# Transposes of B's probabilities put ahead of C's last score product in the mixers' tails, and the experts' gate products run without interruption

## The chip, the cores and the metric

The kernel runs on one core of a Trainium2 chip. The metric is the device time of one execution in microseconds (us). An engine is named by its short name: PE is TensorE (matrix products and transposes), DVE VectorE, ACT ScalarE, POOL GpSimd, SP SyncE, which here only issues DMAs. PSUM is the memory that PE writes its results to; DVE and ACT read them from there.

## The reference: two layers of three attentions and a mixture of experts

The sequence has 256 tokens of width 1024. Each of the two layers does this, all in fp32:

```
mod = silu(c) @ ada_w[l] + ada_b[l]          # six vectors sh1 sc1 g1 sh2 sc2 g2
h = rmsnorm(x) * (1 + sc1) + sh1
proj = h @ w_in[l]                           # columns for three groups of heads
  A: differential attention, 4 heads         # softmax - lam * softmax, then a norm
  B: sliding window of 128, 8 heads on 2 kv heads, with sinks
  C: mixture of three dilated windows, 4 heads
x = x + g1 * (concat(A, B, C) @ w_out[l])
h = rmsnorm(x) * (1 + sc2) + sh2
# router: the best of 4 groups, in it the best 2 of 4 experts, per token
x = x + g2 * sum over the chosen experts of  gate * (silu(h @ wg) * (h @ wu)) @ wd
```

After the layers comes a last norm. There are 16 experts with 1024 x 512 matrices, so the weights (283.63 MB are moved in all) have to come from HBM once.

## The kernel before: one written order for PE, a ring of weight tiles, and a scheduler for the rest

**Weights.** SP issues all weight loads in one fixed sequence (class Ring, the DMAs stand at L154). Most go into 29 buffers of 512 KB called `big`, a few into borrowed `k` or `w` tiles of the kernel's other pools. A load can be issued when the buffer that it goes into has been read by its last user, mostly a PE product, and up to eight loads are under way at a time.

**PE's order is written by hand** (`tc.manual_schedule` for PE). For a mixer it is a string of steps, one list for each layer (MIX), with a common end (TAIL):

- `Pug` is a unit of the projection by w_in, `W0` to `W6` the units of the product with w_out. Both are done as three products of high and low parts of the operands (L724 to L726); ACT makes the high part of a weight by a cast (L776), DVE the low part by a subtraction (L781, one takes 1.2 us).
- For the three groups of heads: `T` transposes queries and keys, `F` makes scores (L1081 for B and C), `V` transposes probabilities (L809), `O` is the product with the values (L890, L893), `AM` transposes A's result (copies L1057, L1058). `CT0` and `CT1` are the transposes of C's queries and keys, whose results ACT and DVE copy (L1074, L1075). `BV0` and `BV1` are the first two transposes of probabilities, `CF0` and `CF1` C's two score steps.
- Behind a score step comes the softmax: DVE masks and takes maxima (L835, reads the scores), negates them (L839, tile `nm`), ACT makes exponentials (L841), DVE takes a reciprocal of the sums (L854) and POOL scales (L857). ACT copies the transposed probabilities (L866) and the products with the values (L896, which W2 needs).
- `a` and `d` are parts of the products of c with ada_w (L462, L537). Of two of these results the columns are taken later by four transposes (L480) and adds (L491 to L494); L551 and L555 are the like for `d`.

The order of DVE, ACT and POOL is not written: a scheduler decides it from PE's order and its own durations. Where two steps share a PSUM buffer (there are two called `t` for transposes and two called `s` for scores), the later one waits until the earlier one has been read.

**The router's bias** is two small products (L603, L604) behind W1, copied by DVE (L606).

**The experts** are done in eight pairs, j = 0 to 7. For an even j, `gather` (L1338) picks the tokens of two pairs by one-hot products in four parts, and ACT and DVE modulate them (L730, L732). For each j come the gate products (L1372, 32 matmuls in four parts of 8), `down` of the pair before (L1418, 32), the up products (L1372, 32), the product of the two (L1403) and `combine` of the pair before (L1439, added to x by L1441). `down_in` is the four transposes (L809) with a copy (L1409) that bring the product into the form that `down` needs. `one_hot` (L1314) makes the one-hot matrices on DVE.

## Time and profile before

| what | value |
|---|---|
| three runs | 746.42, 746.60, 748.49 us (median 746.6) |
| the profiled execution | 746.45 us |
| its span, from the first to the last instruction | 744.6 us |
| busy in the span | PE 708.5 us, DVE 343.4, ACT 213.4, POOL 62.4 |
| moved by DMA | 283.63 MB, 381 GB/s over the span |

The time that lies outside the span is 1.85 us. Layer 0's mixer runs to about 160 us, its experts to 380, layer 1's mixer to about 512, its experts to 730. A view of the timeline lists instructions by their start on one engine, and in brackets how long the engine was idle before and what it waited for; in the chain of waits each line is a stretch of the chain that ended last.

### The profile page before, as it was taken

What the parts mean: (1) busy time and instruction counts of PE and PEld (TensorE: products, weight loads), DVE (VectorE), ACT (ScalarE), POOL (GpSimd) and SP (SyncE); (2) the same over time, 40 slices, a digit from 0 to 9 for tenths busy, and PEclk for the clock granted to TensorE, in tenths of its full rate; (3) what the DMA queues carried; (4) which work ended last, traced back from release to release, by engine and by line L of the source; (5) the groups of instructions that cost most, each with busy time, mean ns of one, the idle gap of its engine ahead of it and who ended that gap; (6) DMA issues with size and microseconds to landing.
All of it is one profiled execution on the core that took longest, in us unless ns stands there. A gap on an engine that the chain in (4) does not pass through costs nothing. (4 is left out here: it accounts for less than half of the span.)

```text
span 744.6 us, 10676 instructions
## 1 busy us (share of the span) xinstructions
PE 708.5 (95%) x3790; PEld 369.1 (50%) x3790; DVE 343.4 (46%) x941; ACT 213.4 (29%) x485; POOL 62.4 (8%) x86
## 2 busy tenths in 40 slices
PE   6899998999999999999999999898999999999993
PEld 2565765764353353353347678575435335344341
DVE  4677796364132233133358879737313312332234
ACT  2445445433111110111134555644211011111012
POOL 1011234001000000000001121400100000000001
PEclk9899999899999999999999999999999999999998
DMA  9999999999989999999999996969899999999991
GB/s 352 409 409 407 407 408 409 407 387 408 406 349 409 409 410 408 409 409 410 399 406 409 405 407 224 354 218 405 315 358 403 406 409 409 409 409 409 409 386 65
DMA packets 82457, 283.63 MB, mean 381 GB/s; under 512 B 9166, under 2 KB 9295, under 8 KB 82396
## 3 DMA queue, kind: packets, MB, share of 16 engines
q1 hardware_dynamic: 82186, 282.85, 96.7%
q8 instruction: 32, 0.52, 0.3%
q14 instruction: 29, 0.24, 0.1%
q0 software_dynamic: 64, 0.02, 0.0%
q10 hardware_dynamic: 146, 0.00, 0.0%
HBM read 281.78 MB, written 1.06 MB: 380 GB/s over the span
## 5 line engine op out<-in xcount | busy, mean ns | idle before, releaser
L1372 PE MATMUL s<-big,k 128*64 128x512 f32 x976 | 228.2, 598 | 0.0
L1372 PEld LDWEIGHTS s<-big,k 128*64 128x64 f32 x976 | 67.3, 136 | 118.6 <-issue 103.8
L1424 DVE SCALAR_TENSOR_TENSOR w<-acc,gs,g 128x512 f32<-128x512 f32 x28 | 21.0, 751 | 155.3 <-PE acc L1418 153.8
L1418 PE MATMUL acc<-big,w 128*64 128x512 f32 x384 | 84.4, 592 | 0.0
L781 DVE TENSOR_TENSOR k<-big,k 128x1024 fp32r<-128x1024 f32 (+1 forms) x56 | 66.8, 1201 | 14.3 <-ACT k L776 10.5
L724 PE MATMUL acc<-k 128*128 128x512 f32 (+1 forms) x176 | 69.9, 397 | 2.9 <-ACT k L713 2.0
L725 PE MATMUL acc<-k 128*128 128x512 f32 (+1 forms) x176 | 66.4, 377 | 0.0
L726 PE MATMUL acc<-k 128*128 128x512 f32 (+1 forms) x176 | 66.4, 377 | 0.0
L776 ACT CAST k<-big 128x1024 fp32r<-128x1024 f32 (+1 forms) x56 | 54.1, 983 | 38.9 <-PE acc L725 27.5
L1418 PEld LDWEIGHTS acc<-big,w 128*64 128x64 f32 x384 | 27.6, 137 | 54.8 <-issue 52.5
L1403 DVE TENSOR_TENSOR w<-w,s 128x512 f32<-128x512 f32 x16 | 11.0, 687 | 82.8 <-PE s L1372 82.8
L1428 ACT CAST w<-w 128x512 fp32r<-128x512 f32 x28 | 17.3, 618 | 89.8 <-DVE w L1424 89.8
L724 PEld LDWEIGHTS acc<-k 128*128 128x128 f32 x176 | 33.8, 192 | 17.9 <-issue 6.9
L841 ACT ACTIVATE w<-w,nm 128x128 f32<-128x128 f32 (+1 forms) x80 | 35.4, 444 | 21.4 <-DVE nm L839 21.4
L1338 PEld LDWEIGHTS t<-w,k 128*128 128x128 f32 x256 | 32.8, 190 | 16.3 <-issue 9.9
L1409 ACT COPY w<-t 128x512 f32<-128x512 f32 x16 | 9.3, 584 | 106.4 <-PE t L809 106.4
L1338 PE MATMUL t<-w,k 128*128 128x256 f32 x256 | 37.6, 291 | 1.7 <-DVE w L1314 1.7
L730 ACT ACTIVATE k<-t,mod,mod 128x256 f32<-128x256 f32 x32 | 16.3, 559 | 77.3 <-PE t L1338 77.3
L726 PEld LDWEIGHTS acc<-k 128*128 128x128 f32 x176 | 33.7, 192 | 7.4 <-DVE k L897 1.4
L809 PE MATMUL t<-cb,w 128*128 128x128 f32 x224 | 35.2, 287 | 2.1 <-ACT w L866 1.1
L725 PEld LDWEIGHTS acc<-k 128*128 128x128 f32 x176 | 33.9, 193 | 5.0
L1441 DVE TENSOR_TENSOR x<-x,acc 128x512 f32<-128x512 f32 x56 | 34.9, 683 | 0.2
(272 smaller groups left out, 851.1 us busy)
## 6 DMA issues: line engine op xcount, KB each, us to landing
big<-in_expert_w_up_dram SPq DMA_DIRECT2D x126, 512.0 KB, 10.2
big<-in_expert_w_gate_dram SPq DMA_DIRECT2D x118, 512.0 KB, 10.2
big<-in_expert_w_down_dram SPq DMA_DIRECT2D x108, 512.0 KB, 10.1
big<-in_ada_w_dram SPq DMA_DIRECT2D x80, 512.0 KB, 10.2
big<-in_w_in_dram SPq DMA_DIRECT2D x32, 512.0 KB, 10.2
big<-in_ada_w_first_dram SPq DMA_DIRECT2D x16, 512.0 KB, 10.2
big<-in_w_out_dram SPq DMA_DIRECT2D x16, 512.0 KB, 9.5
w<-in_expert_w_down_dram SPq DMA_DIRECT2D x20, 256.0 KB, 5.9
```

What stands on the lines that cost most here:

```text
L724: self.nc.tensor.matmul(p, lhsT=xh, rhs=wh, start=start, stop=False)
L725: self.nc.tensor.matmul(p, lhsT=xh, rhs=wl, start=False, stop=False)
L726: self.nc.tensor.matmul(p, lhsT=xl, rhs=wh, start=False, stop=stop)
L776: nc.scalar.copy(hi, w)
L781: nc.vector.tensor_tensor(out=lo, in0=w, in1=hi.bitcast(F32), op=OP.subtract)
L809: self.nc.tensor.transpose(p[:, i], b, self.ident)
L841: nc.scalar.activation(e[:, h], e[:, h], AF.Exp, bias=nm[:, g:g + 1], scale=scale, accum_out=sm[:, g:g + 1])
L1338: nc.tensor.matmul(p[:, kk], lhsT=part[t][:, 2 * k2 + kk], rhs=one[:, t], start=(n == 0), stop=(n == 3))
L1372: nc.tensor.matmul(store[j][64 * u:64 * u + 64, :], lhsT=x[k // 4][:, k % 4, c:c + 64], rhs=w[u][kk], start=(k == 0), stop=(k == KT - 1))
L1418: nc.tensor.matmul(ps[hf][64 * u:64 * u + 64, :], lhsT=act[j][:, f, 64 * u:64 * u + 64], rhs=w[u][hf], start=(f == 0), stop=(f == 3))
L1424: nc.vector.scalar_tensor_tensor(out=ds[-1], in0=p, scalar=gates[j], in1=g[:, 512 * hf:512 * hf + 512], op0=OP.mult, op1=OP.mult)
L1441: nc.vector.tensor_tensor(out=self.x[t][:, c], in0=self.x[t][:, c], in1=p, op=OP.add)
```

## The change

Four things are changed.

- In TAIL, `CT0` and `CT1` leave the tail and go into the string ahead of it (layer 0: behind P40 and P41; layer 1: behind P41 and P43). `CF1` moves from behind W0 to behind `BV0 BV1`. One `d` moves.
- The columns of ada results wait for five flushes instead of two when they belong to the next layer (`later_on`), so layer 0's L480 comes behind W4 instead of W1.
- For the experts, an even j does all four gathers first and then all 32 gate matmuls; `down_in` of a pair runs at the end of its own iteration, behind `combine`, and not between the next pair's gates. j = 0 keeps gathers between gates, and j = 1 keeps `down_in(0)` there.
- `one_hot` for pairs 1, 2, 3 of iterations is issued behind the `places` of the iteration before.

The number of instructions stays the same on every engine.

```diff
 TAIL = """
-CT0 d CT1 d d CF0 AM1 d W0 CF1
-BV0 BV1 W1 BV2 BV3 BO0 BV4 W2 BV5 CV0 W3 BO1 CV1 CV2 W4 CO0 W5 W6
+d d CF0 AM1 d d W0 BV0 BV1 CF1
+W1 BV2 BV3 BO0 BV4 W2 BV5 CV0 W3 BO1 CV1 CV2 W4 CO0 W5 W6
 """
...
-P40 P41 BF1 a P42 AM0 P43 BF2 a a a H2 a
+P40 CT0 P41 CT1 BF1 a P42 AM0 P43 BF2 a a a H2 a
...
-P40 P41 BF1 P42 G2 AM0 P43 BF2 H2
+P40 P41 CT0 BF1 P42 G2 AM0 P43 CT1 BF2 H2
...
-        self.pending.append(lambda: self.pending.append(lambda: self.ada_columns(l, q, rows)))
+        self.later_on(2 if q else 5, lambda: self.ada_columns(l, q, rows))
...
+    def later_on(self, n, f):
+
+        self.pending.append(f if n == 1 else lambda: self.later_on(n - 1, f))
...
             if k2 == 0:
-                if b:
-                    self.one_hot(b)
                 xt[b] = [self.wk.tile([128, 4, S], F32, name="k") for _ in range(2)]
...
-        def gates_of(j, between=None):
-
-            if j % 2:
+        def gates_of(j):
+
+            if j == 0:
+                gather(0, 0)
+                gather(0, 1)
                 first("gate", G, j, 0)
+                gather(0, 2)
                 first("gate", G, j, 1)
-                if between:
-                    between()
+                gather(0, 3)
             else:
-                gather(j // 2, 0)
-                gather(j // 2, 1)
+                for k2 in range(0 if j % 2 else 4):
+                    gather(j // 2, k2)
                 first("gate", G, j, 0)
-                gather(j // 2, 2)
-                if between:
-                    between()
+                if j == 1:
+                    down_in(0)
                 first("gate", G, j, 1)
-                gather(j // 2, 3)
             first("gate", G, j, 2)
             first("gate", G, j, 3)
             silu(j)
...
-            gates_of(j, (lambda: down_in(j - 1)) if j else None)
+            gates_of(j)
...
             places(j)
+            if j in (1, 3, 5):
+                self.one_hot(j // 2 + 1)
...
             elif j:
                 combine(j - 1, *parts)
+                down_in(j)
```

In the order of the changed kernel a line has the number of the new file: L480 to L555 are unchanged, lines of the mixer are 4 higher than here (L781 is L785 there, L835 L839, L841 L845, L866 L870, L896 L900, L1048 L1052, L1075 L1079), lines of the experts 2 higher (L1338 is L1340, L1372 L1374, L1439 L1441).

**End of layer 0's mixer, ACT.** Before, the exponentials of CF1 (L841, four of 128x256) stand ahead of all four copies of BV0 to BV3 (L866), and W2's input (L896) behind these:

```order
57 L776 CAST k<-big 128x1024
58 L841 ACTIVATE w,sm<-w,nm 128x256 x4
59 L866 COPY w<-t 128x512 x4
60 L896 CAST k<-s 128x512
61 L866 COPY w<-t 128x512
```

After:

```order
54 L780 CAST k<-big 128x1024 x2
55 L870 COPY w<-t 128x512 x3
56 L845 ACTIVATE w,sm<-w,nm 128x256 x4
57 L870 COPY w<-t 128x512
58 L900 CAST k<-s 128x512
59 L870 COPY w<-t 128x512
```

Three of the copies have moved ahead of the exponentials, and the exponentials stand nearer to L896.

**Layer 1's mixer, DVE, from P42 on.** Before, the last maxima of BF1 (L835) come first, then one subtraction L781, and then the add L494, which reads the columns of L480:

```order
552 L835 ISA w,mx<-s,cb 128x256
553 L835 ISA mx 128x1
554 L838 TENSOR_TENSOR mx<-mx,sink_339 128x2
555 L623 SCALAR_TENSOR_TENSOR rta<-rya 128x4
556 L781 TENSOR_TENSOR k<-big,k 128x1024
557 L838 TENSOR_TENSOR mx<-mx,sink_339 128x2
558 L839 TENSOR_SCALAR nm<-mx 128x2
559 L624 TENSOR_TENSOR rta<-rta,rma 128x4
560 L494 TENSOR_TENSOR mod_3_4169<-t,cb 128x8
```

After:

```order
547 L628 TENSOR_TENSOR rta<-rta,rma 128x4
548 L629 SCALAR_TENSOR_TENSOR rya<-rta,rya 128x4
549 L785 TENSOR_TENSOR k<-big,k 128x1024
550 L1052 TENSOR_TENSOR w<-w,rya 128x256
551 L1053 TENSOR_TENSOR w<-w,cb 128x256
552 L856 TENSOR_TENSOR sm<-sm,es 128x8
553 L494 TENSOR_TENSOR mod_3_4178<-t,cb 128x8
554 L1079 COPY w<-t 128x2x128
555 L839 ISA w,mx<-s,cb 128x256
```

L494 now has the two products of A's norm (L1052, L1053) ahead of it as well, and BF1's maxima come behind it. Somewhat later in the same order of the changed kernel come the maxima of BF2 (rows 569 on):

```order
563 L858 RECIPROCAL rc<-sm 128x8
564 L785 TENSOR_TENSOR k<-big,k 128x1024
565 L1062 TENSOR_TENSOR w<-t,w 128x2x128
566 L842 TENSOR_TENSOR mx<-mx,sink_339 128x2 x2
567 L785 TENSOR_TENSOR k<-big,k 128x1024 x2
568 L843 TENSOR_SCALAR nm<-mx 128x2 x2
569 L839 ISA w,mx<-s,cb 128x256
570 L839 ISA mx 128x1
571 L1079 COPY w<-t 128x2x128
572 L839 ISA w,mx<-s,cb 128x256
```

Before, two subtractions L781 stand between BF1's maxima and BF2's, and two more behind BF2's; now all four stand ahead of BF2's maxima, three of them in these rows.

**Experts, PE, an even j (here j = 2 of layer 0).** Before:

```order
438 L1439 MATMUL acc<-w 128x512 x8
439 L1338 MATMUL t<-w,k 128x256 x16
440 L1372 MATMUL s<-big,k 64x512 x4
441 L1338 MATMUL t<-w,k 128x256 x8
442 L809 MATMUL t<-cb,w 128x128 x4
443 L1372 MATMUL s<-big,k 64x512 x4
444 L1338 MATMUL t<-w,k 128x256 x8
445 L1372 MATMUL s<-big,k 64x512 x8
446 L1418 MATMUL acc<-big,w 64x512 x16
```

After:

```order
437 L1441 MATMUL acc<-w 128x512 x8
438 L813 MATMUL t<-cb,w 128x128 x4
439 L1340 MATMUL t<-w,k 128x256 x32
440 L1374 MATMUL s<-big,k 64x512 x16
441 L1420 MATMUL acc<-big,w 64x512 x16
```

The work is the same; the gate products (L1372, two trace rows for each of these) now stand in one piece, and the transposes L809 of `down_in` behind `combine` (L1439).

## Rows read from the trace of the kernel before

**Rows 1.** The page: GB/s moved by DMA in 40 slices of 18.6 us.

```profile
GB/s 352 409 409 407 407 408 409 407 387 408 406 349 409 409 410 408 409 409 410 399 406 409 405 407 224 354 218 405 315 358 403 406 409 409 409 409 409 409 386 65
```

**Rows 2.** Stretches: us, busy time by engine (instructions), PE clock, DMA share, GB/s.

```profile
129.60:136.40 6.80, 6.80 (x34) 5.00 (x34) 1.95 (x5) 2.10 (x4) 1.18 (x2) 0.50 1.03 410
...
200.00:220.00 20.00, 20.00 (x106) 9.54 (x102) 7.76 (x15) 4.02 (x8) 0.00 (x0) 1.00 0.89 350
```

**Rows 3.** Timeline of PE, layer 0: W1's start, L480, W2's start.

```profile
123.87 0.47 PE L724 MATMUL acc<-k,w 128*128 128x512 f32 x1
...
128.84 0.66 PE L480 MATMUL t<-cb,w 128*128 128x128 f32 x4 [1.96 <-ACT w L866]
...
135.61 0.78 PE L724 MATMUL acc<-k 128*128 128x512 f32 x1
```

**Rows 4.** Timeline of ACT, layer 0: first exponential of CF1, copies of BV0 and BV1.

```profile
126.24 0.51 ACT L841 ACTIVATE w<-w,nm 128x256 f32<-128x256 f32 x1 [4.39 <-DVE nm L839]
...
128.22 1.04 ACT L866 COPY w<-t 128x512 f32<-128x512 f32 x2
```

**Rows 5.** Timeline of SP's DMA queue, layer 0's experts: two issues in succession.

```profile
200.31 0.33 SPq L154 DMA_DIRECT2D k<-in_expert_w_up_dram  x1
206.09 0.80 SPq L154 DMA_DIRECT2D big<-in_expert_w_up_dram  x2
```

**Rows 6.** Who waited (us, times) for the loads issued from 372 to 385.

```profile
  PEld acc L462: 2.7, 5
```

**Rows 7.** Timeline of PE, layer 1: AM0, CT1, CF0, `d`, W1, BV2, W2.

```profile
461.98 0.38 PE L809 MATMUL t<-cb,w 128*128 128x128 f32 x2
...
467.19 0.63 PE L809 MATMUL t<-cb,w 128*128 128x128 f32 x4 [0.76 <-DVE w L1058]
...
471.00 0.71 PE L1081 MATMUL s<-w 64*128 64x128 f32 x8 [1.33 <-DVE w L1075]
...
472.02 1.06 PE L537 MATMUL acc<-big,cb 128*32 128x512 f32 x8
...
478.67 0.48 PE L724 MATMUL acc<-k,w 128*128 128x512 f32 x1
...
482.60 1.09 PE L809 MATMUL t<-cb,w 128*128 128x128 f32 x8 [0.46 <-ACT w L866]
...
485.83 0.50 PE L724 MATMUL acc<-k 128*128 128x512 f32 x1
```

**Rows 8.** Timeline of ACT, layer 1: the cast ahead of the subtraction L781.

```profile
460.94 1.03 ACT L776 CAST k<-big 128x1024 fp32r<-128x1024 f32 x1
```

**Rows 9.** Timeline of DVE, layer 1.

```profile
462.51 1.22 DVE L781 TENSOR_TENSOR k<-big,k 128x1024 fp32r<-128x1024 f32 x1
...
463.86 0.16 DVE L494 TENSOR_TENSOR mod<-t,cb 128x8 f32<-128x8 f32 x1
...
464.28 0.42 DVE L1048 TENSOR_TENSOR w<-w,rya 128x256 f32<-128x256 f32 x1
```

**Rows 10.** Chain of waits, layer 1's experts, j = 2: start, us, engine, tile, line.

```profile
563.39 1.91 PE t L1338 x16
565.30 1.87 PE s L1372 x8
567.17 1.15 PE t L1338 x8
568.31 0.44 PE t L809 x4
...
571.76 3.58 PE s L1372 x16
...
582.72 7.02 PE s L1372 x32
```

**Rows 11.** Tile `big`, 705 to 722: last loads of up, and time to landing.

```profile
L154 SPq DMA_DIRECT2D big<-in_expert_w_up_dram x2: 327/327/327, 705.0 to 706.3; - x2
...
DMA to landing us min/median/max: 10.2/10.4/10.6
```

**Rows 12.** Timeline, PE's weight loads: the first products with the last of these tiles.

```profile
717.59 0.14 PEld L1372 LDWEIGHTS s<-big,k 128*64 128x64 f32 x2 [0.28 <-issue]
```

## The prediction

> **What bounds the kernel now.** I read the page first, then stretches of the span, then the timelines of the four places that the change touches. PE is busy for 95% of the span, and the weights come at 409 GB/s in most slices [rows 1]: 283.63 MB at that rate are 693 us, so two resources lie within some 50 us of each other, and which one decides differs by stage. The slices show how: up to the 24th (about 440 us) DMA is at its rate but for few gaps, from there to the 30th (about 560) it is not, and behind that it is again. A slice below 409 means that the ring is full and waits for PE.
>
> Three stages follow. In layer 0's experts there is one gap: between the issues at 200.31 and 206.09 SP waits for buffers [rows 5], and from 200 to 220 the rate is 350 [rows 2], so (1 - 350/409) x 20 = 2.9 us of DMA time are lost. Behind it DMA runs without pause until layer 1 starts, and there PE waits for its loads: L462 waits 2.7 us in five pieces [rows 6]. So time that PE gains in layer 0 reaches layer 1 only as far as DMA gets earlier, at most those 2.9 us. From 440 to 560 PE and its helpers decide, and what is gained or lost there shifts both. At the end PE is hardly behind the loads: the last tile of the last up product is issued at 706.3, takes 10.2 to land, and is read at 717.59 [rows 11, 12], a margin of 1.1 us. More than that can't be gained in layer 1's experts.
>
> **Layer 0's tail.** From W1's start to W2's start takes 135.61 - 123.87 = 11.74 us [rows 3]; in layer 1 the same products take 485.83 - 478.67 = 7.16, of which 0.46 is a wait [rows 7]. Two things make the difference of 4.6. PE waits 1.96 us, since the copies of BV0 and BV1 start only at 128.22, behind CF1's exponentials that began at 126.24 [rows 3, 4]. And from 129.6 to 136.4 PE's granted clock is 0.50, the lower of its levels of 1.2 and 2.4 GHz [rows 2]; it fell 0.75 us after that wait.
>
> In the changed order the steps up to W1 are the same products, so W1 starts about where it does, 123.8. The copies of BV0 and BV1 stand ahead of the exponentials, which removes the long wait, and L480 is gone from here. PE then does the 6.7 us of layer 1 (7.16 less 0.46) and would be at W2 at 130.5. ACT is later: CF1's maxima now start behind BV0 and BV1, and the L839 behind DVE's copy of the router bias, which waits for L604 at about 127.2. The exponentials then follow from 127.4, or 128.0 behind BV2's copy. They take 2.0 us (126.24 to 128.22, rows 4's two starts), a copy and the cast for W2 0.6 each: 131.2. So W2 starts near 131.3 and not at 135.61, a gain of 4.3 if the clock stays up. By the cap above 2.9 of them arrive at layer 1; bounds 0 and 4.3. L480 behind W4 is the same four transposes (0.66 at half clock [rows 3]), needed only in layer 1: nothing, and 0.7 at most if something waits for it.
>
> **Layer 1's tail.** Here the waits are short: 0.76 ahead of CT1, 1.33 ahead of CF0, 0.46 ahead of BV2, in all 2.55 [rows 7]. Early CT steps could remove them. But DVE is crowded here, and its new order decides. AM0 starts at 461.98 without a wait [rows 7]. CT0 now occupies one of the two `t` buffers, so AM0 needs the other one, which L494 must have read. L494 stands behind an L781, L1048 and L1049. That L781 needs the cast that ends at 460.94 + 1.03 = 461.97 [rows 8]; with 1.15 for an L781, 0.35 for each of the two (1.22 and 0.42 less the overlap of 0.07) and 0.2 to 0.4 for two small ones and their hand-over, L494 ends at about 464.1 [rows 9]. So AM0 is 2.1 later, of which 0.6 is CT0 itself, moved ahead and not new.
>
> From AM0 to CF0 now pass 471.00 - 461.98 = 9.02, with 0.76 and 1.33 of waits, so 6.93 of products. CT0 (0.6, as CT1) is gone from there and one `d` (0.97, its 1.06 less the overlap) stands behind: 5.4, and PE is ready for CF0 at 469.5. But CF0 needs the `s` buffers, that is BF2's maxima on DVE. After L494 come there a copy and BF1's four maxima (0.35 each, as L1048), three L781 (3.45) and small ones (about 0.8, an estimate from 0.16 for L494's size): 470.1, and then two maxima and a copy: CF0 can start at 471.1, its second half 0.7 later. Before, it started at 471.00 with one `d` left, now two are left. From CF0 to W1 pass 478.67 - 471.00 = 7.67 with one `d`, the CF1 that changes places with BV included; now 0.7 and 0.97 more, so W1 starts at 471.1 + 9.3 = 480.4, 1.8 late. W0's last quarter needs a copy (L546) that now stands behind a reciprocal of CF0's sums; it is due just about in time. Behind W1 the 0.46 wait disappears, since its copy no longer stands behind exponentials: W2 is 1.3 late. I take +1.3. Bounds: -2.55 if none of these DVE waits is real (the three waits vanish), and +3 if the chain slips once more by as much, as it would if L546 came late.
>
> **Experts.** For an even j the pieces now are 1.91 + 1.87 + 1.15 + 0.44 + 1.87 + 1.15 + 3.58 = 11.97 [rows 10]. Afterwards: the transposes 0.44, the gathers between 3.4 (1.91 + 2 x 0.76, the step from 8 to 16) and 3.8 (2 x 1.91), the gate products 7.02 in one piece, as the up products take [rows 10]: 10.9 to 11.3. An odd j has 3.58 + 0.6 (four transposes, as CT1) + 3.58 = 7.8 and becomes 7.5. With j = 2 to 7 that is 2.5 to 4 us a layer. What hides the rest: `down_in` now comes soon after DVE's product of 512 columns (half an L781, 0.6), which `combine`, eight products like a part of the gate (1.87), covers; the copy of its transposes and the modulations (about 0.5, half of rows 4's two copies) alternate on two buffers with gathers of 0.76 and more. Without that cover each of five hand-overs would cost 0.5 and the gain of an even j be gone. In layer 0 DMA takes all of it (rows 6 say that PE waits there anyway): 0. In layer 1 the margin caps it: -1.1, bounds 0 and -1.5, since a piece gained ahead of 560, in j = 1, moves the loads too. `one_hot` a few us earlier on an engine that is idle there: nothing.
>
> **Sum.** 746.45 (the profiled execution: a span of 744.6 and 1.85 around it; 0.15 below the median of the three runs) - 2.9 + 1.3 - 1.1 = 743.75, say 743.8.
>
> **Rivals.**
>
> 1. *The clock falls again in layer 0.* In the new order PE has about 0.8 us of waiting ahead of W2, with twelve transposes of BV2 to BV4 between W1 and W2. In the trace the clock fell behind a wait of 1.96 us and four transposes [rows 2, 3], while layer 1's waits of up to 1.33 brought no fall [rows 7]. If it falls for as long as before, 6.8 us at half speed, up to 3.4 are lost: of the 4.3 only 0.9 stay, and the sum is 746.45 - 0.9 + 1.3 - 1.1 = 745.75. The rows lean against it, the wait being shorter. The Trainium skill ("TensorE: Matmul & The Clock Gate", Part 4 on PE-mode transposes) speaks against the change here: a transpose is not counted as PE being busy as a matmul is, so the change packs steps together that would let the clock fall even without a wait. By that rule the time would be this rival's; no row here shows transposes alone bringing it down.
> 2. *The intended gain in layer 1 arrives.* If DVE keeps up, the three waits vanish: -2.55 for +1.3, and 746.45 - 2.9 - 2.55 - 1.1 = 739.9. Against it is the order of DVE; for it, that each link of my chain is a duration from another moment.
> 3. *Nothing comes out of it.* If the gap at 200 has another cause than PE's lateness (rows 5 show only two issues apart), layer 0's gain stops there: 746.45 + 1.3 - 1.1 = 746.65.
> 4. *Slower.* PE's new wait ahead of CF0 is 471.1 - 469.5 = 1.6 us at its first half and some 0.4 more at the second, and 1.5 ahead of AM0, longer than any that layer 1 has now and as long as the one that preceded layer 0's fall of the clock. If the clock falls there for 6.8 us, dense products run at half speed and lose 3.4: 743.75 + 3.4 = 747.15, and with a fall in layer 0 as well (2.0 less gained) 749.15. It decides where layer 1's tail loses more than layer 0 and the experts gain, 2.9 + 1.1 = 4.0; slower by more than can be told needs 2.24 beyond that.
>
> **How the numbers follow.** 0.3% of 746.6 is 2.24 us, about what a measurement of this kernel can tell from no change. Chances: my forecast 0.47, its own range 742.8 to 745.4 (layer 1's tail from +0.3 to +2.9), so that about 0.33 lies below 744.36; rival 1 0.12, rival 2 0.14, rival 3 0.09, rival 4 0.18, of it 0.06 near 747.2, within the border, and 0.12 above 748.84 for a fall in both tails or a fall and a slip. Faster: 0.14 + 0.33 = 0.47; slower 0.12; the same 0.41. For eight in ten the range has to take in most of rival 2 and the near part of rival 4: 740.2 to 748.3.
>
> **What the changed profile would show.** W1 to W2 in layer 0 in 7 to 8 us with no clock of 0.5 from 125 to 140; 200 to 220 at 400 GB/s or more, and layer 1's P00 2 to 3 us earlier; AM0 and CF0 of layer 1 with waits of 1.5 to 2 us on L494 and on L835, and from AM0 to W2 about 23 us (now 485.83 - 461.98 = 23.85); even j at 11.2 us for gathers and gates; loads landing just when the last up products need them. What would make me wrong: a fall of the clock in either tail, a DVE faster or slower than its rows, or PE waiting for loads in layer 0 in other places than L462.

## The result, and the profile after

The changed kernel took 752.68 us (median of 13 executions, 750.62 to 755.65), the kernel before 747.92 beside it (13 executions): a ratio of 1.0068, 95% interval 1.0053 to 1.0083. The change costs 0.68%, some 5 us; forecast was a gain of 0.36%. The profiled execution took 754.12 us with a span of 752.3, 7.7 more than that of before (744.6); the medians lie 4.8 apart, and single executions of either kernel spread over 5 us and more. In the changed kernel the lines from 580 to 1330 stand four later (L724 is L728, L781 is L785, L839 is L843), L1338 is L1340, L1372 is L1374, L1418 is L1420.

The page: GB/s by slices.

```profile
GB/s 352 410 408 408 407 409 408 409 377 410 391 379 411 409 409 410 408 409 410 396 407 409 407 390 187 301 224 406 304 340 364 412 409 409 409 410 409 409 379 67
```

Against [rows 1] layer 0's gap in the twelfth slice is smaller (379 for 349), and of the slices from 25 to 31 five moved less (the 25th 187 for 224, the 31st 364 for 403); behind them the rate is 409 as before, so what was lost there was not made good. Stretches, with the columns of [rows 2]:

```profile
128.00:131.00 3.00, 2.62 (x25) 1.83 (x25) 1.17 (x9) 2.21 (x8) 0.00 (x0) 1.00 1.02 408
131.00:134.00 3.00, 2.42 (x14) 1.51 (x11) 1.11 (x3) 3.00 (x7) 2.04 (x2) 1.00 1.03 411
...
167.00:170.00 3.00, 3.00 (x16) 2.49 (x17) 3.00 (x11) 1.45 (x4) 0.21 (x1) 0.57 1.03 422
200.00:220.00 20.00, 19.84 (x108) 10.29 (x106) 8.78 (x17) 4.14 (x8) 0.00 (x0) 1.00 0.96 376
...
474.00:477.00 3.00, 3.00 (x19) 0.89 (x18) 1.50 (x11) 3.00 (x15) 0.82 (x1) 0.54 0.99 350
524.00:527.00 3.00, 3.00 (x16) 2.12 (x16) 3.00 (x13) 1.31 (x4) 0.20 (x1) 0.59 0.99 396
```

Layer 0's tail keeps its clock now. Between 30 and 740 us the clock is low at three other places: among the gathers of layer 0 (167) and of layer 1 (524), and in layer 1's tail right behind CF0 (474). The timeline of PE at the places of [rows 3], [rows 7], [rows 10] and [rows 12]:

```profile
124.64 0.50 PE L728 MATMUL acc<-k,w 128*128 128x512 f32 x1
...
132.35 0.50 PE L728 MATMUL acc<-k 128*128 128x512 f32 x1 [0.58 <-ACT k L900]
...
464.21 0.44 PE L813 MATMUL t<-cb,w 128*128 128x128 f32 x2 [1.66 <-DVE mod L494]
...
467.50 1.92 PE L537 MATMUL acc<-big,cb 128*32 128x512 f32 x16
472.39 0.48 PE L1085 MATMUL s<-w 64*128 64x128 f32 x2 [2.97 <-DVE mx L839]
...
474.62 2.96 PE L537 MATMUL acc<-big,cb 128*32 128x512 f32 x16
...
489.92 0.50 PE L728 MATMUL acc<-k 128*128 128x512 f32 x1
...
568.90 0.60 PE L813 MATMUL t<-cb,w 128*128 128x128 f32 x4
569.25 2.16 PE L1340 MATMUL t<-w,k 128*128 128x256 f32 x16
571.57 2.17 PE L1340 MATMUL t<-w,k 128*128 128x256 f32 x16 [0.16 <-ACT k L734]
573.67 7.09 PE L1374 MATMUL s<-big,k 128*64 128x512 f32 x32
580.59 2.75 PE L1420 MATMUL acc<-big,w 128*64 128x512 f32 x12
...
722.09 2.35 PE L1374 MATMUL s<-big,k 128*64 128x512 f32 x8 [0.22 <-DMA big<-in_expert_w_up_dram]
724.64 1.93 PE L1374 MATMUL s<-big,k 128*64 128x512 f32 x6 [0.21 <-DMA big<-in_expert_w_up_dram]
726.51 1.20 PE L1441 MATMUL acc<-w 128*128 128x512 f32 x4
```

W2 of layer 0 starts 3.26 us earlier than in [rows 3], W2 of layer 1 4.09 later than in [rows 7]. The gate products of j = 2 run in one piece. At the end PE waits for the up tiles, where [rows 12] had them just in time. The rows of its products show only 0.2 us of each wait; most of it stands ahead of its weight loads:

```profile
722.08 0.20 PEld L1374 LDWEIGHTS s<-big,k 128*64 128x64 f32 x4 [1.10 <-DMA big<-in_expert_w_up_dram]
...
724.64 0.20 PEld L1374 LDWEIGHTS s<-big,k 128*64 128x64 f32 x4 [1.09 <-DMA big<-in_expert_w_up_dram]
```

SP's queue in layer 1's experts, two rows of before and then two of the changed kernel:

```profile
559.65 2.52 SPq L154 DMA_DIRECT2D big<-in_expert_w_gate_dram  x4
567.19 8.99 SPq L154 DMA_DIRECT2D big<-in_expert_w_down_dram  x8
...
565.32 2.52 SPq L154 DMA_DIRECT2D big<-in_expert_w_gate_dram  x4
575.64 5.12 SPq L154 DMA_DIRECT2D big<-in_expert_w_down_dram  x6
```

The gap of [rows 5] ahead of the gate's loads has a second one behind it, ahead of down's. It was there before, 567.19 - (559.65 + 2.52) = 5.02 us, and is now 575.64 - (565.32 + 2.52) = 7.80. Down's loads wait until 575.64, and the first quarter of j = 2's gate products ends at 573.67 + 1.94 = 575.61 (1.94 is the time of eight such products in the trace of before).

Where the span went, from starts of PE's rows. "Layer 1 starts" is its first product of the norm (line 686 of before, 690 of after). *up* is the first up product of j = 1 in layer 1, *end* the first product of combine(6), which stands behind the last up products.

| stretch | before | after | more |
|---|---|---|---|
| to layer 1's start | 392.43 | 392.39 | -0.04 |
| from there to W2 | 93.40 | 97.53 | +4.13 |
| W2 to *up* | 68.43 | 70.00 | +1.57 |
| *up* to *end* | 164.72 | 166.59 | +1.87 |
| *end* to the span's end | 25.6 | 25.8 | +0.2 |

### The profile page after: what moved, and what is told of

Its sections match the earlier page's. It is cut to its first block, busy times and chain, and to the rows that moved or that the text cites. A ratio compares the mean times of both kernels' runs of the same rounds, so it can differ in the third digit from the quotient of the medians.

```text
span 752.3 us, 10664 instructions
## 1 busy us (share of the span) xinstructions
PE 712.7 (95%) x3790; PEld 374.2 (50%) x3790; DVE 342.9 (46%) x941; ACT 214.2 (28%) x485; POOL 61.7 (8%) x86
## 4 chain that ended last, share of the span: by engine, by line
PE 76%; DMA 14%; DVE 5%; ACT 2%; issue 1%; SPq 0%; DVEq 0%; ACTq 0%
PE s L1374 28%; PE acc L1420 12%; PE acc L728 5%; PE acc L730 4%; PE acc L729 4%; PE t L1340 4%; DMA big<-in_ada_w_dram 4%; PE acc L1441 3%; DMA big<-in_expert_w_down_dram 3%; PE t L813 3%; DMA big<-in_expert_w_up_dram 3%; DMA big<-in_w_in_dram 3%; PE acc L462 3%; DVE k L785 1%; DMA big<-in_w_in_last_dram 1%
## 5 line engine op out<-in xcount | busy, mean ns | idle before, releaser
L1374 PE MATMUL s<-big,k 128*64 128x512 f32 x976 | 229.9, 599 | 0.8 <-DMA big<-in_expert_w_up_dram 0.8
L1374 PEld LDWEIGHTS s<-big,k 128*64 128x64 f32 x976 | 70.9, 137 | 129.9 <-issue 116.7
L1420 PE MATMUL acc<-big,w 128*64 128x512 f32 x384 | 85.2, 592 | 0.0
L785 DVE TENSOR_TENSOR k<-big,k 128x1024 fp32r<-128x1024 f32 (+1 forms) x56 | 66.8, 1202 | 14.2 <-ACT k L780 9.8
L728 PE MATMUL acc<-k 128*128 128x512 f32 (+1 forms) x176 | 69.3, 394 | 3.5 <-ACT k L717 2.0
L1420 PEld LDWEIGHTS acc<-big,w 128*64 128x64 f32 x384 | 28.0, 137 | 55.1 <-issue 48.8
L728 PEld LDWEIGHTS acc<-k 128*128 128x128 f32 x176 | 33.4, 190 | 18.6 <-issue 6.0
L1340 PE MATMUL t<-w,k 128*128 128x256 f32 x256 | 38.6, 301 | 2.5 <-DVE w L1318 1.7
L845 ACT ACTIVATE w<-w,nm 128x128 f32<-128x128 f32 (+1 forms) x80 | 35.3, 443 | 18.2 <-DVE nm L843 18.1
L1340 PEld LDWEIGHTS t<-w,k 128*128 128x128 f32 x256 | 33.9, 198 | 8.2 <-issue 5.2
L1400 ACT ACTIVATE w<-s 128x512 f32<-128x512 f32 x16 | 9.6, 597 | 90.8 <-PE s L1374 90.8
```

Of the source, the lines that this page charges most:

```text
L728: self.nc.tensor.matmul(p, lhsT=xh, rhs=wh, start=start, stop=False)
L785: nc.vector.tensor_tensor(out=lo, in0=w, in1=hi.bitcast(F32), op=OP.subtract)
L845: nc.scalar.activation(e[:, h], e[:, h], AF.Exp, bias=nm[:, g:g + 1], scale=scale, accum_out=sm[:, g:g + 1])
L1340: nc.tensor.matmul(p[:, kk], lhsT=part[t][:, 2 * k2 + kk], rhs=one[:, t], start=(n == 0), stop=(n == 3))
L1374: nc.tensor.matmul(store[j][64 * u:64 * u + 64, :], lhsT=x[k // 4][:, k % 4, c:c + 64], rhs=w[u][kk], start=(k == 0), stop=(k == KT - 1))
L1420: nc.tensor.matmul(ps[hf][64 * u:64 * u + 64, :], lhsT=act[j][:, f, 64 * u:64 * u + 64], rhs=w[u][hf], start=(f == 0), stop=(f == 3))
```

## The experiments

Ratios are to the kernel before on the same chip, with 95% intervals; the last three columns are the stretches of the table above, in us, of each one's profiled execution. One profile differs from the next: the five kernels with layer 0's mixer of before (before, e2, e9, e10, e12) start layer 1 between 392.18 and 393.79.

| kernel | median us | ratio | layer 1 starts | to W2 | *up* to *end* |
|---|---|---|---|---|---|
| before | 747.3 to 748.4 | 1 | 392.43 | 93.40 | 164.72 |
| changed | 752.68 | 1.0068 [1.0053, 1.0083] | 392.39 | 97.53 | 166.59 |
| e1 mixers only | 750.08 | 1.0030 [1.0015, 1.0045] | 391.06 | 98.39 | 164.72 |
| e2 experts only | 749.32 | 1.0022 [1.0004, 1.0039] | 392.44 | 93.42 | 166.67 |
| e3 changed, j = 2 as before | 750.39 | 1.0045 [1.0027, 1.0063] | 390.98 | 98.93 | 164.23 |
| e4 layer 0's tail only | 745.97 | 0.9977 [0.9961, 0.9992] | 390.69 | 93.36 | 164.72 |
| e5 changed, layer 1's tail old | 747.91 | 1.0011 [0.9994, 1.0027] | 390.92 | 93.39 | 166.21 |
| e6 e4 and new experts but j = 2 | 746.17 | 0.9979 [0.9964, 0.9995] | 390.94 | 93.47 | 164.59 |
| e7 e4 and CF1 moved | 745.72 | 0.9983 [0.9968, 0.9997] | 391.65 | 93.32 | 164.71 |
| e8 e1 with CT behind the maxima | 746.62 | 0.9991 [0.9977, 1.0005] | 389.84 | 93.83 | 164.71 |
| e9 j = 2 alone | 748.29 | 1.0001 [0.9985, 1.0017] | 393.79 | 93.35 | 165.08 |
| e10 early release | 750.15 | 1.0030 [1.0013, 1.0046] | 392.18 | 93.36 | 166.56 |
| e11 e6 with early release | 745.91 | 0.9965 [0.9950, 0.9980] | 392.31 | 93.43 | 164.08 |
| e12 early release, no wait | 747.51 | 0.9991 [0.9973, 1.0008] | 393.55 | 94.56 | 164.72 |
| e13 changed, early release | 752.78 | 1.0066 [1.0040, 1.0091] | 392.85 | 99.01 | 166.47 |
| e14 best parts | 745.42 | 0.9971 [0.9956, 0.9986] | 390.34 | 93.36 | 164.07 |
| e15 changed, GpSimd later | 753.59 | 1.0071 [1.0046, 1.0097] | 392.54 | 99.08 | 166.28 |
| e16 e14, GpSimd later | 745.08 | 0.9973 [0.9955, 0.9990] | 390.38 | 93.40 | 163.76 |
| e17 changed, two multiplications out | 750.63 | 1.0036 [1.0021, 1.0052] | 392.44 | 96.22 | 165.94 |

**The change in halves.** e1 has the hunks on `TAIL`, `MIX` and `later_on` alone, and `moe` as before; e2 has those in `moe` alone. Against the changed kernel, in their core:

```diff
 e1
-                for k2 in range(0 if j % 2 else 4):
-                    gather(j // 2, k2)
                 first("gate", G, j, 0)
...
 e2
-d d CF0 AM1 d d W0 BV0 BV1 CF1
-W1 BV2 BV3
+CT0 d CT1 d d CF0 AM1 d W0 CF1
+BV0 BV1 W1 BV2 BV3
...
-P40 P41 CT0 BF1 P42 G2 AM0 P43 CT1 BF2 H2
+P40 P41 BF1 P42 G2 AM0 P43 BF2 H2
```

> The mixers' strings and the later columns as changed, the experts as before. Theory of the late release (the changed experts use the gate tiles of j = 2 some 2.3 us later behind combine, so their buffers come free later and DMA stands still 2.8 us longer in each layer): without that, DMA's gap at 200 to 210 us closes by about 2.9 us, layer 1 starts 2 to 3 us earlier, and loses 2.7 to 4.1 at its W2; total 0 to +1.2 us against the kernel before. Rival (the experts are harmless, layer 1's tail is to blame for all): +4 to +6 us.

> The mixers as before, only the experts' order as changed. Theory of the late release: from the last load of a gate to the first of down of the next pair DMA's queue is still for 7.8 us instead of 5.0, in both layers; layer 1 starts 2.5 us later, and the whole is 4 to 5.5 us slower. Rival (the experts are harmless): between -1.1 and 0 us.

Both halves cost, 0.30% and 0.22%. e1 loses 5 us between layer 1's start and W2 and nothing in the experts; e2 the reverse. The rival for e1, that the tail is what costs, has the place right though not the size (1.0030 is some 2.3 us); in e2 late loads cost less than expected.

e3 puts the gathers of j = 2 back between the gate products, in the changed kernel; e4 takes from the change only layer 0's strings and the later columns (layer 1's strings and `moe` are those of before):

```diff
 e3
-            if j == 0:
-                gather(0, 0)
-                gather(0, 1)
+            if j in (0, 2):
+                gather(j // 2, 0)
+                gather(j // 2, 1)
...
 e4
-""" + TAIL).split()]
+""" + TAIL_OF_BEFORE).split()]
```

> The changed kernel, but in the pair j = 2 the gathers stand between the gate products as in the kernel before (its transposes of the pair before stay behind combine). Theory of the late release: j = 2 is the only pair for which the ring is full, so nearly all of the experts' loss goes: the gap in front of the loads of down is back at about 5.5 us, and the time is 4 to 5 us below the changed kernel's, 0 to +1.2 us against the kernel before. Rival (layer 1's tail alone): as the changed kernel, +5.

> The new strings and later columns in layer 0's mixer alone, layer 1's mixer and all experts as before. Theory of the late release: W2 of layer 0 is 3.3 us earlier, the gap in DMA at 200 to 210 closes by as much, layer 1 starts 2.5 to 2.9 us earlier and the whole is that much faster, 744. Rival (layer 0's gain is lost there for another reason, such as the clock that fell at its gathers): 746 to 747, no change.

e3's median gets back 0.23% of 0.68% (the two intervals overlap a little), and *up* to *end* is even shorter than before: that part of the loss hangs on j = 2. What stays is layer 1's tail, larger than expected. e4 is a gain: 0.23%, some 1.7 us; layer 1 starts 1.74 earlier and nothing of it is lost behind.

**Layer 1's tail.** e5 is the changed kernel with layer 1's strings of before (e2's last edits, in layer 1 alone). e6 is e4 and the experts' new order except in j = 2 (e3's edit). e7 is e4 with one move in layer 1, e8 is e1 with the CT steps of layer 1 put behind BF2's maxima:

```diff
 e7
-CT0 d CT1 d d CF0 AM1 d W0 CF1
-BV0 BV1 W1 BV2
+CT0 d CT1 d d CF0 AM1 d W0 BV0 BV1 CF1
+W1 BV2
 e8
-P40 P41 CT0 BF1 P42 G2 AM0 P43 CT1 BF2 H2
+P40 P41 BF1 P42 G2 AM0 P43 BF2 CT0 H2 CT1
```

> The changed kernel with layer 1's steps in their old order; layer 0's tail, the later columns and the experts stay as changed. Theory (the changed kernel loses at two places: layer 1's tail, where VectorE's new order and the wait ahead of CF0 cost some 4 us, and the experts, whose gathers in one piece let the loads out later): the tail's 4 us come back, W2 of layer 1 starts near 484 to 486 instead of 489.92, and what stays is the experts' loss: 3 to 5 us below the changed kernel, 0 to +1.5 against the kernel before. Rival (layer 1's tail costs only what a fall of the clock that wanders from place to place costs, and the fall goes elsewhere): at most 1.5 us below the changed kernel.

> The kernel before with two parts of the change: layer 0's new tail with the later columns, and the experts' new order for all experts but j = 2, whose gathers stay between the gate products. Theory (it is the gathers of j = 2 in one piece that let buffers come free late, in both layers, when loads are due): the loss of the experts is gone, and the kernel is as the one with layer 0's tail alone or up to 1 us faster: -1.5 to -2.5 against the kernel before. Rival (any gathers in one piece, or the steps down_in placed behind combine, cost it): 1.5 to 2.5 above the kernel with layer 0's tail alone, so 0 to +1 against the kernel before.

> The kernel before with layer 0's new tail and columns, and in layer 1 one move alone: CF1 goes behind BV0 and BV1, while the CT steps stay in the tail. Theory (the CT steps ahead of the last fill are what layer 1's tail pays for, by VectorE's order ahead of BF2's maxima): AM0 starts without a wait, CF0 waits 1.3 us as before, W2 of layer 1 is where it was against AM0 or 0.5 earlier: -1.5 to -2.5 against the kernel before. Rival (exponentials behind BV1 are what makes CF1 and W2 late): W2 1 to 2 us later against AM0 than before, and the kernel within 0.5 of the one before.

> The changed mixers with the experts of before, but in layer 1 CT0 and CT1 stand behind BF2 and H2 instead of ahead of BF1 and BF2, so that VectorE takes the maxima of BF2 before the copies of the CT steps and AM0 needs no buffer that CT0 holds. Theory (VectorE's order makes the two new waits of 1.7 and 3.0 us, and the clock falls behind the second): AM0 starts without a wait, CF0 waits under 1.5 us, no fall of the clock right behind it, layer 1's tail is within 1 us of before, and the kernel is 2.5 to 4 us below the one with all mixers changed: 0 to -2 against the kernel before. Rival (the products left behind CF0 and the three steps d there cost it, whatever VectorE does): within 1.5 us of the kernel with all mixers changed, +1 to +2.2 against before.

In e5 the loss of 0.68% is 0.11%: layer 1's tail is most of it, and the old strings need 93.39 us from start to W2 as before. e7 shows that CF1 behind BV1 costs nothing (93.32). So it is the CT steps put ahead of BF1 and BF2, and e8 shows that it is their place ahead of the maxima, not the two `d` behind CF0 (one before; its expectation counts three): with the CT steps behind the maxima and the same two `d` the tail takes 93.83 instead of e1's 98.39. e8's PE at AM0 and CF0:

```profile
464.58 0.63 PE L813 MATMUL t<-cb,w 128*128 128x128 f32 x4 [1.75 <-DVE w L1062]
465.14 1.92 PE L537 MATMUL acc<-big,cb 128*32 128x512 f32 x16
468.40 0.71 PE L1085 MATMUL s<-w 64*128 64x128 f32 x8 [1.34 <-DVE w L1079]
```

The wait of 1.34 ahead of CF0 is that of [rows 7]; AM0 ran at 459.38 without a wait, and the other wait stands ahead of CT1, where [rows 7] have 0.76. The granted clock is 1.00 throughout this tail. e6 is like e4: the new order of the pairs other than j = 2 costs nothing, and gains nothing that can be told.

**What the experts lose.** e9 does j = 2's one piece alone, in the kernel before. e10 does the opposite in the kernel before: it lets the first quarter of j = 2's gate products, and with it the buffers, come earlier. e11 is e6 with that edit.

```diff
 e9
+            if j == 2:
+                for k2 in range(4):
+                    gather(1, k2)
+                first("gate", G, j, 0)
+                between()
+                first("gate", G, j, 1)
 e10
                 first("gate", G, j, 0)
+                if j == 2:
+                    combine(0, *parts)
                 gather(j // 2, 2)
 ...
-            elif j:
+            elif j > 1:
                 combine(j - 1, *parts)
```

> The kernel before with one edit: the gathers of j = 2 stand ahead of its gate products in one piece, with down_in(1) between the first two gate parts. Theory (the end of the first gate part of j = 2 frees the buffers that the loads of down wait for; what delays that part delays the loads, at a time when the loads set the end): that part ends some 2 us later, SyncE issues the loads of down 2 us later in both layers, and the kernel is 1 to 2 us above the kernel before, like the one with all experts changed. Rival (the loss of the changed experts comes from the steps of j = 4 and 6, or from the clock): within 0.7 us of the kernel before.

> The kernel before with the opposite edit: combine(0), some 2 us of products that stand ahead of the gathers of j = 2, goes behind the first gate part of j = 2; no work is added or taken away. Theory: that part ends 2 us earlier, SyncE issues the loads of down 2 us earlier (at about 215.1 and 565.2 where the kernel before has 217.06 and 567.19), the gap in the loads from 200 to 220 shrinks from 2.95 us to about 1, and layer 1 starts 1 to 2 us earlier: 0.5 to 2 us below the kernel before. Rival (the order of work inside the same pair of experts changes nothing, since the sum of PE's work is the same): within 0.5 us of the kernel before.

> Layer 0's new tail, the experts' new order for j = 1 and 3 to 7, and for j = 2 combine(0) behind the first gate part. Theory (the gain of PE in the experts of layer 1 was not to be seen because the loads were as late as before): the loads now come 2 us earlier in both layers, the gap of 1.2 us that is left from 200 to 220 goes, and with it up to 1.1 us of PE's gain: 0.5 to 1.5 us below the kernel with layer 0's tail and the same experts, 2 to 3 below the kernel before. Rival (what is left at the end is limited by the whole of the loads behind the slack stretch from 440 to 560, which this does not shorten): within 0.5 us of the kernel with layer 0's tail and the same experts.

e9 shows no difference that can be told (its interval reaches to +0.17%), and *up* to *end* grows by 0.36 only: alone, the one piece does not cost what it does among the changed experts. e10 was not clean: PE waited 1.24 us for the one-hot tile ahead of the gathers, and it is slower. e11, where that tile is made early, is 0.14% below e6, less than the intervals part. e12 is e10 with the early tile, e13 has the edit in the changed kernel, e14 joins e11 and e7:

```diff
 e12
-                if b:
+                if b > 1:
                     self.one_hot(b)
 ...
             places(j)
+            if j == 1:
+                self.one_hot(1)
 e13
+                if j == 2:
+                    combine(0, *parts)
+                    gather(1, 2)
+                    down_in(1)
+                    gather(1, 3)
```

> The kernel before with combine(0) behind the first gate part of j = 2, and the one-hot tile of j = 2 made during j = 1, so that the gathers don't wait for it. Theory (the end of that gate part frees the buffers for the loads of down, and that sets when loads come in both layers): it ends some 2 us earlier against the up products of j = 1 (10.9 us behind their start instead of 12.9), PE's pace stays, the loads of down are issued 2 us earlier: 0.5 to 1.5 us below the kernel before. Rival (what counts is the end of the last gate part, that is PE's pace as a whole, and the first release is hidden): within 0.5 us of the kernel before.

> The changed kernel, with two gathers of j = 2, combine(0) and down_in(1) behind the first gate part of j = 2. Theory: the loads of down are issued some 4.5 us earlier against PE than in the changed kernel, and 1.5 to 3 us of its loss come back, as with the gathers of j = 2 interleaved or somewhat more: 749.5 to 751, +2 to +3.5 against the kernel before, all of it layer 1's tail. Rival (late loads are not what the experts cost): within 0.7 us of the changed kernel, +4.5 to +5.5 against the kernel before.

> The parts that gained or cost nothing, together: layer 0's new tail, in layer 1 CF1 alone moved behind BV1, the experts' new order but for j = 2, where combine(0) stands behind the first gate part. Theory: as the same kernel without CF1's move, or up to 0.5 us faster: 2 to 3.5 us below the kernel before. Rival (the parts share one slack, and together give no more than layer 0's tail alone): 1.2 to 1.8 us below the kernel before.

e13 goes against the theory: SP's queue and PE in layer 1,

```profile
571.39 11.42 SPq L154 DMA_DIRECT2D big<-in_expert_w_down_dram  x8
583.72 5.77 SPq L154 DMA_DIRECT2D big<-in_expert_w_up_dram  x7
```

```profile
575.46 1.21 PE L1340 MATMUL t<-w,k 128*128 128x256 f32 x8 [0.67 <-ACT k L734]
576.61 5.37 PE L1374 MATMUL s<-big,k 128*64 128x512 f32 x24
```

Down's loads are issued 571.39 - 560.30 = 11.09 us behind *up*, in the changed kernel 575.64 - 559.92 = 15.72, and yet the loss stays (166.47). In e9 they are issued at 570.89, 15.27 behind *up* and so nearly as late as in the changed kernel, and hardly anything is lost. So the first quarter's end does not set it by itself. In e13 the eight issues take 11.42 us, and the other three quarters start at 576.61, 16.31 behind *up* (in the changed kernel 575.61, 15.69 behind), 0.67 of it a wait for ScalarE.

What goes along with the loss is the time that DMA loses in all around this place. From 5 us ahead of *up* to 50 behind it, before and in the changed kernel:

```profile
549.26:604.26 55.00, 55.00 (x270) 22.70 (x268) 14.88 (x28) 7.31 (x14) 0.00 (x0) 1.00 0.98 388
...
554.92:609.92 55.00, 54.84 (x272) 23.15 (x270) 14.90 (x28) 7.43 (x14) 0.00 (x0) 1.00 0.94 370
```

Against 409 GB/s these are 2.8 and 5.2 us lost. The same stretch has 370 to 379 in the six profiles whose *up* to *end* is 1.2 to 1.95 us longer than before (changed, e2, e5, e13, e15, e17), and 382 to 390 in all others but e10 (378, with its own wait), which are 0.36 longer at most. So the experts' loss goes with late loads; which buffer's release makes them late is not settled.

e12 is at 164.72 and not to be told from before. e14 gains 0.29%, with *up* to *end* at 164.07, with e11's 164.08 the least but for e16.

**VectorE and GpSimd.** In the changed kernel two multiplications of GpSimd lie ahead of BF2's maxima. They scale the probabilities by the reciprocals of their sums. e15 has the sums and reciprocals for them behind these maxima in the program, e16 the same in e14, and e17 leaves the two multiplications out (the probabilities of BF0 in layer 1 stay unnormalised):

```diff
 e15, e16
-            if n != 1:
+            if n == 0 and l == 1:
+                T["br"] = rest
+            elif n != 1:
+                if n == 2 and l == 1:
+                    T["bp", 0] = T.pop("br")()[0]
                 T["bp", t] = rest()[0]
 e17
-                T["bp", t] = rest()[0]
+                T["bp", t] = rest(l == 0 or t == 1)[0]
 ...
-            if whole:
+            if whole and times:
```

> The changed kernel with one edit in layer 1: the sums, the reciprocal and GpSimd's two multiplications for BF0's probabilities stand behind BF2's maxima instead of right behind BF0. Theory (VectorE's operations on two tensors wait while GpSimd multiplies, and that is the 1.3 us that the prediction's chain lacked): the two L785 ahead of BF2's maxima take 2.3 us instead of 3.21, the maxima start some 1.3 us earlier, CF0 waits 1.6 us instead of 2.97, and 1.3 us come back, 1.4 to 2.8 more if the clock now stays up behind that wait: 1.3 to 4 us below the changed kernel. Rival (the long operations have another cause, or the multiplications cost the same at their new place): CF0 waits 2.5 us or more, within 0.7 us of the changed kernel.

> The version of the best parts with the same edit in layer 1. Theory: VectorE is rid of 1.3 us ahead of BF2's maxima, CF0's wait of 1.3 us goes for the most part, layer 1's W2 comes about 1 us earlier, and all behind it: 1 us below the version without it, 3 to 4 us below the kernel before. Rival (the multiplications delay something else, BV0's transposes or CF0's exponentials, by as much): within 0.5 us of the version without it.

> The changed kernel without GpSimd's two multiplications of BF0's probabilities by the reciprocals of their sums in layer 1 (256 rows of the output's attention B stay unnormalised; PE's, VectorE's and ScalarE's work is the same). Theory (VectorE's operations wait for GpSimd's): BF2's maxima start at about 470.0 instead of 471.24, CF0 at 471.1 with a wait of 1.6 to 1.7 us instead of 2.97, as the prediction's sum had it; if the fall of the clock needs the long wait, it is gone as well: W2 of layer 1 1.3 us earlier, or 2.7 to 4 with the clock. Rival (the long operations have another cause): CF0 waits 2.5 us or more as in the changed kernel, and the time is within 0.7 us of it.

VectorE in the changed kernel from the third subtraction to the first of BF2's maxima:

```profile
465.88 1.18 DVE L785 TENSOR_TENSOR k<-big,k 128x1024 fp32r<-128x1024 f32 x1
466.97 0.42 DVE L1062 TENSOR_TENSOR w<-t,w 128x256 fp32r<-128x256 f32 x1
467.31 0.74 DVE L842 TENSOR_TENSOR mx<-mx,sink 128x2 f32<-128x2 f32 x2
467.97 3.21 DVE L785 TENSOR_TENSOR k<-big,k 128x1024 fp32r<-128x1024 f32 x2
471.10 0.23 DVE L843 TENSOR_SCALAR nm<-mx 128x2 f32<-128x2 f32 x2
471.24 0.41 DVE L839 CUSTOM_DVE_ANT_0 w<-s,cb 128x256 f32<-128x256 f32 x1
```

GpSimd beside it:

```profile
466.20 2.76 POOL L861 TENSOR_TENSOR w<-w,rc 128x512 f32<-128x512 f32 x2 [10.08 <-ACT k L780]
```

The same stretch of VectorE in e17, and PE behind it:

```profile
467.33 0.22 DVE L842 TENSOR_TENSOR mx<-mx,sink 128x2 f32<-128x2 f32 x2
467.47 2.35 DVE L785 TENSOR_TENSOR k<-big,k 128x1024 fp32r<-128x1024 f32 x2
469.74 0.23 DVE L843 TENSOR_SCALAR nm<-mx 128x2 f32<-128x2 f32 x2
469.88 0.41 DVE L839 CUSTOM_DVE_ANT_0 w<-s,cb 128x256 f32<-128x256 f32 x1
```

```profile
471.04 0.48 PE L1085 MATMUL s<-w 64*128 64x128 f32 x2 [1.59 <-DVE mx L839]
...
472.73 3.44 PE L537 MATMUL acc<-big,cb 128*32 128x512 f32 x16
...
488.66 0.50 PE L728 MATMUL acc<-k 128*128 128x512 f32 x1
```

Without GpSimd's work the two tiny L842 take 0.22 instead of 0.74 and the two subtractions 2.35 instead of 3.21, the maxima start 1.36 earlier, and CF0 waits 1.59 us. e17's median is 1.0036 of the kernel before, the changed one's 1.0068: some 2.4 us, more than the 1.3 at this place, and what the rest is was not looked for. In e15 the multiplications moved by only 1.69, since the scheduler drew the reciprocal forward; there two tiny L843 took 1.00 each, and CF0 was no earlier. VectorE and then GpSimd:

```profile
467.58 1.17 DVE L785 TENSOR_TENSOR k<-big,k 128x1024 fp32r<-128x1024 f32 x1
468.67 1.00 DVE L843 TENSOR_SCALAR nm<-mx 128x2 f32<-128x2 f32 x1
469.59 1.21 DVE L785 TENSOR_TENSOR k<-big,k 128x1024 fp32r<-128x1024 f32 x1
470.73 1.00 DVE L843 TENSOR_SCALAR nm<-mx 128x2 f32<-128x2 f32 x1
...
467.89 3.81 POOL L861 TENSOR_TENSOR w<-w,rc 128x512 f32<-128x512 f32 x2 [11.67 <-ACT k L780]
```

The second L843 ends at 471.73, GpSimd's second multiplication at 467.89 + 3.81 = 471.70. So e15 told nothing apart by its time, but it shows the loss going along with GpSimd to whichever operation of VectorE stands beside it. In e16 the multiplications moved by no more than the kernel around them (462.58 for 462.51 in e14), and it is e14 again. The Trainium skill ("SBUF — State Buffer", section "SBUF: two separate sides") says that VectorE and GpSimd share one pair of ports as a lock that one instruction holds to its end; the rows of e15 and e17 agree with that.

In e17 the clock fell all the same behind CF0: the sixteen products of `d` take 3.44 us where 1.92 is their time at full clock. The fall does not need the long wait. It is there in all six profiles with the changed kernel's strings in layer 1 and in none of the thirteen with others; e8, with waits of 1.75 and 1.34 close together, has none. What brings it is left open.

## Why the prediction was wrong

**Layer 0's tail, forecast -2.9 at layer 1.** The mechanism was right, its size was not. W1 to W2 takes 132.35 - 124.64 = 7.71 us (forecast "7 to 8"), the clock stays up, and W2 is 3.26 earlier where 4.3 was summed; W1 itself came 0.8 later than summed. That both the wait and the clock cost there shows in e10, which has the old tail without a fall: 9.87 from W1 to W2, against 11.1 to 12.1 in the four old tails with one (before, e2, e9, e12). Rival 1 did not come true: in none of the fourteen profiles with the new tail does the clock fall behind W1's start (in four it fell ahead of it, at 122.6 to 123.4). The Trainium skill's rule on transposes that was cited there ("TensorE: Matmul & The Clock Gate", Part 4) is not borne out by the twelve, with some products among them, between W1 and W2. (L480's 0.66 was read as being at half clock; the row ends ahead of 129.6, where the clock fell. Nothing in the sum hangs on it.) By itself this part is worth 0.23%, 1.7 us (e4). The cap of 2.9 was taken as the gain, while the lead does not arrive whole: in nine of the fourteen profiles layer 1 starts 0.8 to 2.6 us earlier, in five (changed, e11, e13, e15, e17) not by more than 0.12. In the changed kernel none arrived: of 3.26, 1.57 was left at j = 1's up products (204.13 to 202.56) behind the fall of the clock at 167, and from 200 to 220 loads ran at 376 GB/s, not the 400 forecast. It took both the fall and the new experts' late loads: e1, with the fall and the experts of before, starts layer 1 at 391.06, and e5, with the same layer 0 as the changed kernel but no fall, at 390.92, each some 1.4 to 1.5 earlier than before.

**Layer 1's tail, forecast +1.3, measured +4.1.** This is the step that failed most, and the sum can be followed link by link. AM0 at 464.21 (464.1), PE ready for CF0 at 469.42 (469.5): right. CF0 at 472.39 for 471.1: the link "three L781 (3.45) and small ones" priced every operation by its undisturbed row, and left out the 1.3 us for which GpSimd holds VectorE up. The trace of before has the like, and the prediction passed it over: the subtraction that was priced at 1.15 takes 2.09 there beside GpSimd.

```profile
464.62 2.09 DVE L781 TENSOR_TENSOR k<-big,k 128x1024 fp32r<-128x1024 f32 x1
...
464.58 3.02 POOL L857 TENSOR_TENSOR w<-w,rc 128x512 f32<-128x512 f32 x2 [8.42 <-ACT k L776]
```

e17, where they are gone, has the maxima at 469.88 (forecast 470.1) and CF0 at 471.04 with a wait of 1.59 (forecast 1.6). The other 1.5 are the clock: 3.44 - 1.92 in e17's `d` (in the changed kernel the clock is low from CF0 on, at 473.4, and `d` behind it takes 2.96). In e17, 96.22 - 93.40 = 2.8 less 1.5 leaves 1.3, the forecast. So the sum was right for what it held, and lacked GpSimd (1.3) and rival 4's fall (1.5 here; 3.4 was its price, for 6.8 us at half clock, and the fall here lasted 3.4). In four of the six profiles with these strings (e1, e3, e13, e15) it does last 6.8, and layer 1's start to W2 is 98.4 to 99.1.

**The experts, forecast -1.1, measured +1.9.** PE does gain: layer 0's up products from j = 1 to j = 7 come 1.6 us closer (157.70 to 156.06), less than the 2.5 to 4 summed, as the 32 gathers need 573.67 - 569.25 = 4.42 and not 3.4 to 3.8; in three pieces they took 1.91 + 1.15 + 1.15 = 4.21 [rows 10]. But the gain never reaches the end, since the loads come later and PE waits for them at 722.09 and 724.64. The step that failed is the term -1.1, "in layer 1 the margin caps it": it took the loads' times as fixed, where they hang on when the gate products free buffers, and the gathers in one piece put all four quarters' start behind 4.4 us. The prediction read one gap in SP's queue [rows 5]; the second one, ahead of down's loads, is the one that grew, from 5.02 to 7.80. What is shown: with all experts changed *up* to *end* is 1.2 to 1.95 us longer (changed, e2, e5, e15, e17), and with j = 2 put back it is not (e3, e6); and DMA's rate around *up* goes with it in every profile but e10's. Which of the four quarters decides is not shown: j = 2 alone cost 0.36, and e13's early first quarter gave nothing back.

**Not foreseen.** A fall of the clock among layer 1's gathers, 1.57 in this profile. It does not go with the change's parts: e2, e4, e6, e11, e14 and e16 have one there, the others have none. Without it the profiled execution would be about 752.5, near the median.

**The cases.** Slower had 0.12, by rival 4 with a second mishap. Its mechanism, the clock at CF0, took part with 1.5 us; the rest came from GpSimd beside VectorE, which stands only among its signs of being wrong ("a DVE faster or slower than its rows"), and from the loads of layer 1's experts, which stand in no case. The range ended at 748.3, since neither GpSimd beside VectorE nor loads that wait for the gate products had a bound.

## What to carry to other kernels

A chain of VectorE's operations is not the sum of their undisturbed rows: where GpSimd works beside it, take the long rows. Where loads fill a ring of buffers, moving products that read it later within a block moves the loads, even if the block gets shorter; ask when each buffer is freed before counting PE's gain. What holds of this change is layer 0's tail (0.23% by itself); with the experts' new order for j = 1 and 3 to 7 and combine(0) behind j = 2's first quarter (e11, e14, e16) it is 0.27 to 0.35%, which the intervals do not part from 0.23.

## What the runs showed of the hardware

The granted clock falls to its lower level, 1.2 GHz, for some 3.4 or 6.8 us at a time at places that differ from one kernel's profile to another's though the code there is the same. In the tail of layer 0, with the new order, it is low between 122.6 and 126.8 in four profiles (e3, e4, e6, e11) and not at all in ten; with the old order between 128.6 and 136.4 in four (before, e2, e9, e12) and not at all in e10. Each fall costs 1.3 to 1.6 us of PE's time per 3.4. Most of the spread of one kernel goes along with this: of 35 executions of the kernel before, the seven with a mean granted clock of 0.990 or more took 744.87 to 745.98 us, the seven with 0.983 or less 748.97 to 750.26. A single profile therefore can't tell 2 us.

VectorE's operation on 2 elements a partition took 1.00 us beside GpSimd and 0.16 without: the size of an operation does not bound what such a meeting costs it.
